# A hybrid decoder step on one Trainium2 core: the attention stage and the samples' decode attention put into one stated order of small pieces

## The chip, the cores and the metric

The program runs on 1 core of one Trainium2 chip. The metric is the device time of one execution in microseconds (us), lower is better. TensorE is PE in the profile (PEld is its weight load, which overlaps its matmuls), VectorE is DVE, ScalarE is ACT, GpSimd is POOL and SyncE, which here issues most of the DMAs, is SP.

## The reference

One inference step of a two-layer trunk for a prompt of 512 tokens and 8 samples of one token, with shared weights: layer 0 is native sparse attention, layer 1 an mLSTM. What matters here is layer 0:

```
h = rmsnorm(x);  q, kv, win, gates, z = split(h @ w_in)          # 16 heads of 64, 4 kv heads
o_c = softmax(q kc - slope*d) vc        # compressed keys (31 of the prompt, 63 of a sample)
o_s = softmax(q ks - slope*d, selected blocks) vs
o_w = softmax(q kw - slope*d, window 512) vw
o   = g0*o_c + g1*o_s + g2*o_w
x   = x + (o * silu(z)) @ w_out
```

For the prompt of 512 tokens all 8 selection blocks fall within the 16 that may be selected, so both the selection and the window branch are causal attention over 512 rows. A sample attends to 1024 rows out of paged memory (128 rows a page, 8 pages, found through a page table) in the selection branch and to 512 rows of a window cache in the window branch.

## The kernel before, in words

All is float32. A product that needs full accuracy is three float32r matmuls on a high and a low part (`mm3`, lines 255 to 258). `load_w` (271) is how a weight comes in: SP issues its DMA into one of 2 `wraw` buffers, ACT copies the high part (276), `lo_of` (253) subtracts it on DVE or POOL.

The stages of layer 0 are: the k and v projections with the samples' compressed keys (up to about 235 us), the q tiles (`q_tile`, 651), the gate tiles z (`z_tile`, 677, to about 331 us), the attention (331 to 524 us), the output projection (lines 1085 to 1101). PSUM has 8 banks: 2 named mm, 3 named s, 2 named t and 1 named d.

**The prompt's attention** is 32 units (line 992): 2 head pairs hp, 4 groups g, and 4 row blocks i in the order 1, 3, 0, 2, each with 128(i+1) keys, 2 branches and 2 heads. For each of these 4 combinations `sub_a` (915) makes the scores with two matmuls (926, 927) into an s bank, DVE adds the distance and takes the extreme (929), ACT takes the exponential (931). `stats` (935) makes the 4 factors on DVE. `sub_b` (941) scales the scores on DVE (945), transposes them on PE (949) into an s or a t bank and copies them to SBUF (951 on ACT, 953 on DVE). `sub_pv` (959) multiplies all with the values in one run of matmuls (974), 2(2i+3) of them, into an mm bank. After the fourth unit of a (hp, g), `finish` (982) applies z and splits the result. `pair_start` (862) makes the compressed branch of a (hp, g): 8 matmuls (870), a softmax on DVE and ACT, a multiply on the engine that `PMUL` names (888), 2 transposes (891).

The loop at 1002 writes this down by hand: in step k it alternates the four `sub_a` of unit k with the four `sub_b` of unit k-1, and puts the value run of unit k-2 after the second of them. The compiler's scheduler then orders the instructions of each engine, by priority. The value runs and the samples' runs have a raised priority (`burst`, 708) and stay behind the newest score product; the first matmul of a value run waits for all four copies of its unit (969 to 972).

**The samples' decode attention** is a generator (`decode`, 716) that the loop advances by one piece in most steps (`DECP`, 1025): 12 score pieces (774, 32 matmul instructions each), a softmax over 1536 columns (779 to 801), three pieces for the compressed and the new rows, 12 value pieces (806, 16 instructions each, after a transpose at 811, a copy at 814 and a zeroing on POOL at 813), and the closing (839 to 848). Each score or value piece needs a block of 1 MB in one of 2 `dk` buffers. `fetch` (693) has SP issue it: 8 DMAs of one page each, each after a read of the page table (`pages`, 406), or one DMA for a window block. Three score pieces come in the z stage, at k = 3, 5 and 7; the generator's opening (the samples' compressed branch) and the fetch of block 0 come at k = 1 there, behind the load of z weight 2.

SP's instructions are in the order of the program up to line 1106. The first two output weights are loaded in steps 26 and 28 (`WOP`, 1027). After the loop the samples' result is put into the 8 operands of the output projection, by 8 copies on ACT (1030) and 8 subtractions on DVE. Then ACT issues the four loads of x for the residual (1053).

A class `Plan` (144) is used by two later stages, from about 731 us on. `P.op(engine, us, due, fn, ...)` notes a piece of one engine with what it reads and writes, and `P.run(order)` calls the pieces in the order of a tuple of numbers, within a block in which the scheduler keeps that order on all five engines:

```
    def run(self, order):
        gone = set()
        for k in order:
            fn, deps = self.ops[k]
            assert deps <= gone, k
            gone.add(k)
            fn()
```

The us and due of a piece are kept out of the program: only the order remains.

Of the kernel before, what the change touches and what calls it, by code (L numbers as in the profile page):

```python
# [32 lines left out]
LO_S = "VVVVVVVVVVVVVVVV"  # L33
# [6 lines left out]
PMUL = "VGGVVVVV"  # L40
# [5 lines left out]
WOP = (26, 28)  # L46
DECP = (0, 1, 1, 0, 1, 1, 0, 1, 1, 0, 1, 1, 0, 1, 1, 0, 1, 1, 0, 1, 1, 0, 1, 1, 0, 1, 1, 0, 1, 1, 1, 0, 1)
SBUFS = 7
PTB = 8
BURST = 4000  # L50
# [15 lines left out]
CS0, CSP = 6.0, 10.0  # L66
ORDER0 = (
# [17 lines left out]
ORDER1 = (  # L85
# [55 lines left out]
class Plan:  # L141
# [27 lines left out]
    def run(self, order):  # L169
        assert sorted(order) == list(range(len(self.ops)))  # L170
# [3 lines that stand above are left out]
            assert deps <= gone, k  # L174
            gone.add(k)
            fn()

# [33 lines left out]
def step_kernel(ctx, tc, ap):  # L211
# [479 lines left out]


# [13 lines left out]
    tail = []  # L706

    def burst(head):

        ctx_ = ExitStack()  # L710
        if tail:
            ctx_.enter_context(tc.high_priority(offset=BURST))
            ctx_.enter_context(tc.issue_after(head or tail[-1]))
        return ctx_

    def decode():
# [16 lines left out]
        pcm = d1.tile([128, 128], F32, name="dpc")  # L733
# [25 lines left out]
        V.tensor_reduce(st[:, 3:5], sn, axis=AX.X, op=OP.add)  # L759

        nxt = fetch(0)
        for u in range(12):
            yield
            cur, nxt = nxt, fetch(u + 1)
            dst = db()
            cs = slice(0, 128)
            kt = cur.rearrange("p b (h t) -> p b h t", h=2)
            head = None
            for par in (1, 0):
                for hp in range(2):  # L770
                    for cg in (3, 2, 1, 0):
                        b = 2 * cg + par
                        with burst(head):
                            m = PE.matmul(dst[32 * cg:32 * cg + 32, cs], QZ[:, hp, b], kt[:, b, hp],
                                          start=par == 1 and hp == 0, stop=par == 0 and hp == 1)
                        head = head or m.ins
            V.tensor_add(PS[:, u * 128:(u + 1) * 128], PS[:, u * 128:(u + 1) * 128], dst[:, cs])
        mn = d1.tile([128, 4], F32, name="dmn")
        V.tensor_reduce(mn[:, 0:1], PS[:, 0:1024], axis=AX.X, op=OP.min)
        V.tensor_reduce(mn[:, 2:3], PS[:, 1024:1536], axis=AX.X, op=OP.min)  # L780
        V.tensor_tensor(mn[:, 0:1], mn[:, 0:1], st[:, 3:4], op=OP.min)
        V.tensor_tensor(mn[:, 1:2], mn[:, 2:3], st[:, 4:5], op=OP.min)
        sm = d1.tile([128, 4], F32, name="dsm")
        pnw = d1.tile([128, 2], F32, name="dpn")
        S.activation(PS[:, 0:1024], PS[:, 0:1024], AF.Exp, scale=-1.0, bias=mn[:, 0:1], accum_out=sm[:, 0:1])
        S.activation(PS[:, 1024:1536], PS[:, 1024:1536], AF.Exp, scale=-1.0, bias=mn[:, 1:2], accum_out=sm[:, 1:2])
        V.tensor_sub(pnw, mn[:, 0:2], st[:, 3:5])
        S.activation(pnw, pnw, AF.Exp)
        V.tensor_add(sm[:, 0:2], sm[:, 0:2], pnw)
        V.tensor_scalar(sm[:, 0:2], sm[:, 0:2], 1e-30, None, op0=OP.max)  # L790
        V.reciprocal(sm[:, 0:2], sm[:, 0:2])
        V.tensor_mul(sm[:, 0:2], sm[:, 0:2], GD[:, 1:3])
        V.tensor_mul(pnw, pnw, sm[:, 0:2])
        V.tensor_scalar(PS[:, 0:1024], PS[:, 0:1024], sm[:, 0:1], None, op0=OP.mult)
        V.tensor_scalar(PS[:, 1024:1536], PS[:, 1024:1536], sm[:, 1:2], None, op0=OP.mult)
        V.tensor_scalar(pcm[:, 0:64], pcm[:, 0:64], GD[:, 0:1], None, op0=OP.mult)
        V.tensor_copy(pcm[:, 64:128], pcm[:, 0:64])
        pno = d1.tile([128, 2, 8], F32, name="dpo")
        for i in range(2):
            V.tensor_scalar(pno[:, i], C("bmask"), pnw[:, i:i + 1], None, op0=OP.mult)  # L800

        po = db()

        def pv_mm(lhs, rhs, b, start, stop):
            cg, s_ = b % 4, b // 4
            return PE.matmul(po[32 * cg:32 * cg + 32, s_ * 256:s_ * 256 + 256], lhs, rhs, start=start and s_ == 0,  # L806
                             stop=stop, skip_group_check=True)

        def p_nat(src, n):
            pp = xb()  # L810
            PE.transpose(pp[0:n, 0:128], src, ident)
            d = dp.tile([128, 8, 32], F32, name="dpt", tag="dpt")
            G.memset(d, 0.0)
            V.tensor_copy(d[0:n, :, 0:16], pp[0:n, 0:128].rearrange("p (b h) -> p b h", b=8))
            return d

        pc_ = p_nat(pcm, 128)
        for s_ in range(2):
            for cg in range(4):
                b = s_ * 4 + cg  # L820
                r = slice(64 * (b % 2), 64 * (b % 2) + 64)
# [75 lines left out]
    for k in range(8):  # L897
# [3 lines left out]
        if k % 2:  # L901
            next(dec)
# [1357 lines left out]
```

## Time and profile before

| | |
|---|---|
| time, median of 3 runs (lowest to highest) | 1162.23 us (1158.26 to 1164.24) |
| the profiled execution | 1153.69 us, its span 1152.0 us |
| granted clock, mean over the span | 0.976 |
| PE busy | 1069.0 us, 93% of the span |
| PEld, DVE, ACT, POOL busy | 82%, 70%, 54%, 23% |
| moved by DMA | 197.20 MB, 171 GB/s |
| the attention stage | 331 to 524 us |

A busy PE isn't a PE at its peak: matmuls are pipelined, each is shown for some 0.27 us and more, and the next starts well before that ends. A short wait between two matmuls therefore doesn't show as idle time of PE; the weight loads (PEld) show it. The view of the waits names for each engine the line that sat idle and the one that ended it; "issue" is a wait that the profile doesn't explain.

### The profile page before, as it was taken

What the parts mean: (1) busy time and instruction counts of PE and PEld (TensorE: products, weight loads), DVE (VectorE), ACT (ScalarE), POOL (GpSimd) and SP (SyncE); (2) the same over time, 40 slices, a digit from 0 to 9 for tenths busy, and PEclk for the clock granted to TensorE, in tenths of its full rate; (3) what the DMA queues carried; (4) which work ended last, traced back from release to release, by engine and by line L of the source; (5) the groups of instructions that cost most, each with busy time, mean ns of one, the idle gap of its engine ahead of it and who ended that gap; (6) DMA issues with size and microseconds to landing.
All of it is one profiled execution on the core that took longest, in us unless ns stands there. A gap on an engine that the chain in (4) does not pass through costs nothing.

```text
span 1152.0 us, 24275 instructions
## 1 busy us (share of the span) xinstructions
PE 1069.0 (93%) x8673; PEld 939.0 (82%) x8673; DVE 806.9 (70%) x1972; ACT 617.4 (54%) x1304; POOL 262.8 (23%) x296
## 2 busy tenths in 40 slices
PE   5899999999998999998899899898989999999985
PEld 4899999999987767678898899688956677877885
DVE  6675564487567888785777667585666778778786
ACT  5533444444566767673444344566665656655544
POOL 5021212043200000111543222231231233322111
PEclk9998999999999999999999999899999999999998
DMA  6544455023434433525444333679868787978522
GB/s 214 170 152 151 125 163 161 30 60 127 145 93 131 138 93 117 191 90 181 132 141 138 129 115 127 219 172 308 284 227 294 255 285 251 341 239 310 180 80 90
DMA packets 124754, 197.20 MB, mean 171 GB/s; under 512 B 16205, under 2 KB 66254, under 8 KB 124378
## 3 DMA queue, kind: packets, MB, share of 16 engines
q1 hardware_dynamic: 115930, 180.52, 48.8%
q10 hardware_dynamic: 8704, 15.13, 3.6%
q8 instruction: 68, 1.11, 0.4%
q14 instruction: 52, 0.43, 0.1%
HBM read 145.89 MB, written 58.10 MB: 177 GB/s over the span
## 4 chain that ended last, share of the span: by engine, by line
PE 60%; DVE 15%; DMA 9%; ACT 8%; issue 5%; SPq 2%; POOL 0%; DVEq 0%; ACTq 0%; POOLq 0%
PE mm L256 11%; PE mm L258 11%; PE mm L257 10%; DMA wraw<-in_m_in 4%; PE mm L974 3%; PE s L1817 3%; PE d L1453 2%; ACT pt L951 2%; PE s L257 2%; PE s L258 2%; PE s L256 2%; ACT s L931 2%; ACT whi L276 1%; PE t L949 1%; PE d L806 1%
## 5 line engine op out<-in xcount | busy, mean ns | idle before, releaser
L256 PE MATMUL mm<-hhi,whi 128*128 128x260 f32 (+1 forms) x976 | 284.3, 291 | 18.6 <-ACT hhi L314 9.7
L258 PE MATMUL mm<-hhi,wlo 128*128 128x260 f32 (+1 forms) x976 | 279.8, 287 | 5.1 <-DVE wlo L253 5.1
L257 PE MATMUL mm<-hlo,whi 128*128 128x260 f32 (+1 forms) x976 | 279.1, 286 | 0.0
L256 PEld LDWEIGHTS mm<-hhi,whi 128*128 128x128 f32 (+1 forms) x976 | 185.6, 190 | 27.0 <-issue 11.0
L253 POOL TENSOR_TENSOR wlo<-wraw,whi 128x1024 fp32r<-128x1024 f32 (+2 forms) x57 | 116.9, 2051 | 332.9 <-ACT whi L276 188.3
L258 PEld LDWEIGHTS mm<-hhi,wlo 128*128 128x128 f32 (+1 forms) x976 | 185.5, 190 | 6.9 <-DVE wlo L253 6.7
L257 PEld LDWEIGHTS mm<-hlo,whi 128*128 128x128 f32 (+1 forms) x976 | 185.6, 190 | 0.5
L276 ACT ACTIVATE whi<-wraw 128x1024 fp32r<-128x1024 f32 (+2 forms) x62 | 61.6, 993 | 106.8 <-DMA wraw<-in_m_in 46.6
L1472 DVE SCALAR_TENSOR_TENSOR cs<-t,wk,cs 128x512 f32<-128x512 f32 x128 | 88.4, 744 | 13.7 <-PE t L1445 10.2
L257 PE MATMUL s<-plo,w1h 128*128 128x256 f32 x256 | 73.7, 288 | 4.4 <-DVE plo L253 4.2
L1467 ACT ACTIVATE cs<-cs,SBC 128x1024 f32<-128x1024 f32 x64 | 70.7, 1141 | 12.5 <-PE d L1453 12.5
L931 ACT ACTIVATE s<-s,mn 128x256 f32<-128x256 f32 (+3 forms) x128 | 70.9, 555 | 11.1 <-DVE mn L929 7.8
L253 DVE TENSOR_TENSOR wlo<-wraw,whi 128x1024 fp32r<-128x1024 f32 (+1 forms) x44 | 48.9, 1114 | 39.2 <-ACT whi L276 33.1
L256 PE MATMUL s<-phi,w1h 128*128 128x256 f32 x256 | 76.0, 297 | 0.0
L258 PE MATMUL s<-phi,w1l 128*128 128x256 f32 x256 | 72.8, 284 | 0.0
L929 DVE CUSTOM_DVE_ANT_0 s<-s,D 128x256 f32<-128x256 f32 (+3 forms) x128 | 61.3, 486 | 10.0 <-PE s L927 7.1
L256 PE MATMUL mm<-uh,whi 128*128 128x260 f32 x224 | 66.1, 295 | 0.3 <-ACT sq L1927 0.2
L253 DVE TENSOR_TENSOR plo<-praw,phi 128x1024 fp32r<-128x1024 f32 x31 | 40.4, 1305 | 34.7 <-ACT phi L426 21.5
L257 PE MATMUL mm<-ul,whi 128*128 128x260 f32 x224 | 63.5, 284 | 0.0
L258 PE MATMUL mm<-uh,wlo 128*128 128x260 f32 x224 | 63.5, 284 | 0.0
L257 PEld LDWEIGHTS s<-plo,w1h 128*128 128x128 f32 x256 | 48.9, 191 | 5.5 <-DVE plo L253 5.0
L926 PE MATMUL s<-KA,qst 128*128 128x256 f32 (+3 forms) x128 | 49.1, 387 | 1.4 <-DVE mn L929 1.1
(472 smaller groups left out, 2723.4 us busy)
## 6 DMA issues: line engine op xcount, KB each, us to landing
cs<-in_state_C SPq DMA_DIRECT2D x64, 512.0 KB, 5.3
o_cs<-cs SPq DMA_DIRECT2D x64, 512.0 KB, 4.3
praw<-in_cache SPq DMA_DIRECT2D x128, 128.0 KB, 2.4
dk<-in_cache SPq DMA_DIRECT2D x128, 128.0 KB, 2.3
wraw<-in_m_in SPq DMA_DIRECT2D x32, 512.0 KB, 4.5
wraw<-in_m_out SPq DMA_DIRECT2D x32, 256.0 KB, 3.8
wraw<-in_w_kv SPq DMA_DIRECT2D x11, 512.0 KB, 3.4
wraw<-in_w_q SPq DMA_DIRECT2D x8, 512.0 KB, 3.4
```

The source lines that it names most:

```text
L253: (eng or V).tensor_sub(out, src, hi.bitcast(F32))
L256: PE.matmul(out, whi, xhi, start=start, stop=False)
L257: PE.matmul(out, whi, xlo, start=False, stop=False)
L258: PE.matmul(out, wlo, xhi, start=False, stop=stop)
L276: S.activation(hi, raw, AF.Copy)
L926: PE.matmul(p[:, 0:n], q[:, h2, i * 128:(i + 1) * 128], KA[:, kh, o:o + n], start=True, stop=False)
L929: V.tensor_tensor_reduce(s[:, 0:n], p[:, 0:n], D0[:, 384 - 128 * i:512], SLOPES[4 * kh + g], CLAMP, op0=OP.add, op1=OP.min, accum_out=mn[: ...
L931: S.activation(s[:, 0:n], s[:, 0:n], AF.Exp, scale=-1.0, bias=mn[:, h2, br:br + 1], accum_out=sm[:, h2, br:br + 1])
L974: m = PE.matmul(po[64 * h2:64 * h2 + 64, ts], lhs, rhs, start=n == 0, stop=n == len(todo) - 1)
L1467: S.activation(ct, ct, AF.Copy, scale=SBC[:, hd, 0, b:b + 1])
L1472: V.scalar_tensor_tensor(ct[:, i], D["pb_", k], D["wk_", hd][:, 2 * kh + i, b:b + 1], ct[:, i], op0=OP.mult, op1=OP.add)
L1817: PE.matmul(st_out(hd, j), ct[:, ks], X["q"][:, 128 * j:], start=kt == 0 and j < 3, stop=kt == 3, skip_group_check=True)
```

## The change

The prompt's attention, the samples' attention from their score piece 3 on, the loads of the first two output weights and the samples' 16 closing operations become 1054 pieces: 345 of PE, 390 of DVE, 275 of ACT, 22 of POOL and 22 of SP. `ORDER0` states them in one sequence; the former `ORDER0` and `ORDER1` are now `ORDER1` and `ORDER2` and are not changed. `DECP`, `WOP`, `burst`, the raised priority and the added waits at the head of a value run are gone. `PMUL` gives two more of the eight multiplies of the compressed branch to POOL. The number of buffers, the matmuls and the operations stay as they are. The opening of the decode attention and the fetch of block 0 come before the z tiles, ahead of the load of z weight 1.

```diff
-PMUL = "VGGVVVVV"
+PMUL = "VGGVGVGV"
-WOP = (26, 28)
-DECP = (0, 1, 1, 0, 1, 1, 0, 1, 1, 0, 1, 1, 0, 1, 1, 0, ...
-BURST = 4000
+AB, AS, AV = 4.0, 1.0, 5.0
+AL = {0: 3.4, 1: 4.6, 2: 6.0, 3: 7.4}
+DL0, DS0, DP0, DPS = 0.0, 78.0, 90.0, 7.0
 ORDER0 = (
+    8, 948, 950, 912, 954, 11, 9, 14, 913, 12, 10, 15, 13, 16, 17, 914, 34, 18, 63, 35, 19, 43, 20, 36, 37, 44,
+    21, 45, 40, 24, 27, 22, 30, 0, 41, 23, 38, 42, 25, 28, 1, 31, 26, 29, 2, 69, 32, 39, 60, 33, 3, 61, 921, 46,
...
+class _Now:
+    def op(self, eng, us, due, fn, **kw):
+        fn()
...
+    def dec_load(P, u, due):
+        D["dk", u] = Tile_("dk")
+        def load():
+            D["dk_", u] = fetch(u)
+        pages_ = u % 12 < 8
+        P.op("SP", 9.4 if pages_ else 0.4, due, load, new=[D["dk", u]], mb=0.13 if pages_ else 1.05)
+    def dec_qk(P, u, due):
...
+        P.op("PE", 1.3, due, run, r=[t], new=[dst])
+        P.op("DVE", 0.2, due + 1.3, add, r=[dst], w=[("PS", u)])
...
-    dec = decode()
+    N = _Now()
+    dec_open()
+    dec_load(N, 0, 0)
     for k in range(8):
         if k < 7:
             wz.append(load_w(ap["w_z"][k + 1], 8, eng=E[LO_Z[k + 1]]))
         z_tile(k, wz[k])
-        if k % 2:
-            next(dec)
+        if k in (3, 5, 7):
+            u = k // 2 - 1
+            dec_load(N, u + 1, 0)
+            dec_qk(N, u, 0)
         if k == 6:
-            for _ in pair_start(0, 0):
-                pass
+            pair_start(N, 0, 0, 0)
...
+    def att_unit(P, hp, g, i, due):
...
+                P.op("PE", TA[n], d, prod, r=[qt], new=[pt_])
+                P.op("DVE", TT[n] + 0.01, d + 0.6, dist, r=[pt_] + ([] if f0 else [mn]), w=[(mn, key)],
+                     new=[st] + ([mn, sm] if f0 else []))
+                P.op("ACT", TE[n], d + 1.4, ex, r=[(mn, key)], w=[st, (sm, key)])
...
+        P.op("DVE", 0.26, b_ - 0.5, stats, r=[(sm, k_) for k_ in sp_], w=[sm], lock=True)
...
+                P.op("DVE", TS[n], d, scale, r=[sm], w=[st])
+                P.op("PE", 0.11 * (i + 1) + 0.02, d + 0.5, tr, r=[st], new=[pb_])
+                P.op("ACT" if PTC[2 * i + h2] == "S" else "DVE", TC[n], d + 1, copy, r=[pb_], new=[pt_])
...
+        P.op("PE", 0.228 * (2 * i + 3) + 0.15, b_ + AV, pv, r=list(pts.values()) + [D["ptc", hp, g]], w=[] if f else [po],
+             new=[po] if f else [])
...
-    for k in range(len(units) + 1):
...
+    P = Plan({"mm": 2, "s": 3, "t": 2, "d": 1, "dk": 2, "qo": 9, ...
+    for k, (hp, g, i) in enumerate(units):
+        if k % 4 == 0 and k + 4 < 32:
+            pair_start(P, *units[k + 4][:2], at_ + 6)
+        att_unit(P, hp, g, i, at_)
+        at_ += AL[i]
+    end_ = at_
+    for u in range(3, 12):
+        dec_load(P, u + 1, DL0 + 9.6 * (u - 3))
+        dec_qk(P, u, DL0 + 2 + 9.0 * (u - 3))
+    dec_soft(P, DS0)
+    dec_first(P, DS0 + 6)
+    for u in range(12):
+        if u < 11:
+            dec_load(P, 13 + u, DL0 + 9.6 * (u + 9))
+        dec_pv(P, u, DP0 + DPS * u)
+    dec_close(P, DP0 + DPS * 12 + 2)
+    for k in range(2):
+        wo_load(P, k, end_ - 20 + 8 * k)
...
+    for k in range(8):
+        P.op("ACT", 0.1, end_ + 2.5 + 0.2 * k, lambda k=k: samp_h(k), r=["us", D["uo", k]], w=[("uos", k)])
+        P.op("DVE", 0.08, end_ + 3 + 0.2 * k, lambda k=k: samp_l(k), r=["us", (D["uo", k], 1), ("uos", k)], lock=True)
+    with tc.manual_schedule(engines=every):
+        P.run(ORDER0)
```

What the sequence says can be read from the numbers, since pieces are numbered in the order in which they are noted. Counted in that way: the value run of a unit has 2 to 25 other PE pieces between itself and the last of the unit's transposes, 8 in the median; a unit's first transpose piece has 4 to 13 other PE pieces between itself and its last score product, 8 in the median. One of the three s banks is taken 192 times; 38 of these takes stand at most 5 places (of all engines) behind the piece that empties the bank, the median 7. The page blocks of the scores are fetched and used in the order 4, 7, 5, 6, 10, 8, 11, 9. The loads of output weights 0 and 1 stand behind the fetch of block 10, and ACT's copies of their high parts 12 and 21 PE pieces after these loads. The 8 ACT copies of the samples are the last ACT pieces, behind the split of the last unit.

## Rows read from the trace of the kernel before

**Rows 1.** Stages: us, busy PE, PEld, DVE, ACT, POOL, clock, DMA share, GB/s.

```profile
331.00:524.00 193.00, 175.17 (x1982) 138.91 (x1982) 154.29 (x637) 133.62 (x413) 13.17 (x19) 0.99 0.39 122
740.00:846.00 106.00, 100.42 (x786) 90.77 (x785) 68.17 (x127) 68.57 (x131) 25.53 (x32) 0.98 0.79 244
846.00:1075.00 229.00, 224.14 (x1306) 166.29 (x1305) 174.37 (x356) 137.24 (x223) 66.22 (x80) 0.99 0.84 284
```

**Rows 2.** Waits of PEld, 331 to 524: us in total, times, longest.

```profile
PEld mm L974 <- ACT pt L951: 14.1, 21, 1.1
PEld t L949 <- issue: 5.8, 16, 1.2
PEld s L926 <- DVE mn L929: 4.1, 13, 1.1
PEld t L949 <- DVE s L945: 3.9, 7, 1.6
PEld t L949 <- PE d L806: 2.5, 5, 0.8
```

**Rows 3.** The chain that ended last: start, us, what (count includes both passes).

```profile
392.01 0.50 ACT pt L951
392.55 2.19 PE mm L974 x36
394.74 1.01 PE d L774 x32
...
436.06 0.81 PE t L870 x8
...
445.54 1.00 PE d L806 x16
...
459.46 1.31 PE mm L974 x20
...
461.77 0.60 PE t L949 x4
```

**Rows 4.** Timeline of PE: score products of 256 and of 512 keys.

```profile
331.14 0.28 PE L927 MATMUL s<-KB,qst 128*128 128x256 f32 x1
...
331.37 0.28 PE L927 MATMUL s<-KB,qst 128*128 128x256 f32 x1
...
333.51 0.39 PE L927 MATMUL s<-KB,qst 128*128 128x512 f32 x1
...
333.96 0.40 PE L927 MATMUL s<-KB,qst 128*128 128x512 f32 x1
```

**Rows 5.** Groups of instructions, 331 to 524: busy, mean ns | idle before.

```profile
L256 PE MATMUL mm<-uo,whi 128*128 128x260 f32 x7 | 2.2, 310 | 0.0
...
L276 ACT ACTIVATE whi<-wraw 128x1024 fp32r<-128x1024 f32 x2 | 2.1, 1058 | 1.8 <-DMA wraw<-in_w_o 1.7
...
L1030 ACT ACTIVATE uo<-us 128x8 fp32r<-128x8 f32 x8 | 1.0, 196 | 0.0
```

**Rows 6.** Timelines of SP (merged issues) and of ACT: start, us.

```profile
263.08 11.81 SPq L274 DMA_DIRECT2D wraw<-in_w_z  x3
...
287.65 8.21 SPq L410 DMA_DIRECT2D dk<-in_cache  x8
...
395.81 78.09 SPq L410 DMA_DIRECT2D dk<-in_cache  x64
...
276.74 1.06 ACT L276 ACTIVATE whi<-wraw 128x1024 fp32r<-128x1024 f32 x1
```

**Rows 7.** DMA issues: KB each, median us from issue to landing.

```profile
dk<-in_cache SPq DMA_DIRECT2D x96, 128.0 KB, 2.3
...
wraw<-in_w_q SPq DMA_DIRECT2D x8, 512.0 KB, 3.4
```

**Rows 8.** Timeline behind the attention: ACT's queue, and PE.

```profile
524.56 1.79 ACTq L1053 DMA_DIRECT2D x<-in_xT  x4
...
528.88 0.39 PE L256 MATMUL mm<-uo,whi 128*128 128x260 f32 x1 [1.01 <-DVE x L1091]
```

More of the change, by code (lines that the diff above doesn't have):

```diff
@@ L772, in decode @@
                         b = 2 * cg + par
[L773 to L779, printed above, removed]
@@ L796, in decode @@
[L796 to L807, printed above, removed]
@@ new lines, in pv_mm, with p_nat, tr, zero @@
+    def pv_mm(lhs, rhs, b, start, stop):
+        cg, s_ = b % 4, b // 4
+        return PE.matmul(D["po_"][32 * cg:32 * cg + 32, s_ * 256:s_ * 256 + 256], lhs, rhs, start=start and s_ == 0,
+                         stop=stop, skip_group_check=True)
+    def p_nat(P, key, src, n, due, r):
+        pp, d = Tile_("t"), Tile_("dpt")
+        D["dpt", key] = d
+        X = {}
+        def tr():
+            X["pp"] = xb()
+            PE.transpose(X["pp"][0:n, 0:128], src(), ident)
+        def zero():
+            D["dpt_", key] = dp.tile([128, 8, 32], F32, name="dpt", tag="dpt")
+            G.memset(D["dpt_", key], 0.0)
+        def put():
+            V.tensor_copy(D["dpt_", key][0:n, :, 0:16], X["pp"][0:n, 0:128].rearrange("p (b h) -> p b h", b=8))
+        P.op("POOL", 0.32, due - 2, zero, new=[d])
+        P.op("PE", 0.13, due, tr, r=r, new=[pp])
+        P.op("DVE", 0.2, due + 0.4, put, r=[pp], w=[d])
@@ L896, in step_kernel, with f1 @@
-    dec = decode()
+        X = {}
+        pcm, s, mc, pp, ptc = Tile_("t"), Tile_("sc"), Tile_("mc"), Tile_("t"), Tile_("ptc")
+        D["ptc", hp, g], D["pov", hp, g] = ptc, Tile_("mm")
+        def f1():
+            q = qst[hp, g]
+            X["p"] = xb().rearrange("p (h i n) -> p h i n", h=2, i=4)
+            for h2 in range(2):
+                for i in range(4):
+                    PE.matmul(X["p"][:, h2, i], q[:, h2, i * 128:(i + 1) * 128], KQ[:, 2 * hp + h2], start=True,
+                              stop=True)
@@ new lines, in f_h, with f_l @@
+        def f_h():
+            uo[k] = qop.tile([128, 2, NTOK], F32R, name="uo", tag="qo")
+            S.activation(uo[k][:, 0, 0:512], X["u"], AF.Copy)
+        def f_l():
+            lo_of(uo[k][:, 1, 0:512], X["u"], uo[k][:, 0, 0:512], E[LO_UO[k]])
+        P.op("DVE", 0.6, b_ + AV + 2, f_u, r=[po], new=[u])
+        P.op("ACT", 0.5, b_ + AV + 3, f_h, r=[u], new=[o])
+        e = LO_UO[k]
+        P.op(EN[e], WLO[e][0], b_ + AV + 4, f_l, r=[u, o], w=[(o, 1)], lock=True)
+    units = [(hp, g, i) for hp in range(2) for g in range(4) for i in IORD]
@@ L1379, in head_factor @@
         V.tensor_mul(out, v, r)
-    EN = {"V": "DVE", "G": "POOL"}
-    WLO = {"V": (0.68, 1.23), "G": (1.28, 2.4)}
-    CTI = [Tile_("big") for _ in range(16)]
-    VTI = [[Tile_("big") for _ in range(4)] for _ in range(4)]
-    D = {}
     def head_open(P, hd, due):
@@ L1727, in step_kernel @@
     with tc.manual_schedule(engines=every):
-        P.run(ORDER0)
+        P.run(ORDER1)
     r1.close()
@@ L2121, in step_kernel @@
     with tc.manual_schedule(engines=every):
-        P.run(ORDER1)
+        P.run(ORDER2)
     kctx.close()
```

493 lines of the change are left out of this document (282 added, 211 removed), and 48 rows, old and new, of the table ORDER0.

## The prediction, made before the changed kernel ran

> **What bounds the kernel now.** I read the table of stages first. In the 193.0 us of the attention PE is busy 175.17, DVE 154.29, ACT 133.62, POOL 13.17 us, at a granted clock of 0.99 (the 2.4 GHz level) [rows 1]: no engine is full, and PE is the fullest. In the two stretches that already run in a stated order PE is busy 100.42 of 106.0 and 224.14 of 229.0 us [rows 1], 95% and 98%, against 91% here.
>
> Busy time hides short waits, so I count PE's work from the steps between starts. A value run takes 2.19 us for 9 pairs of matmuls and 1.31 for 5 [rows 3], 0.22 a pair and 0.21 on top: 0.87, 1.31, 1.75, 2.19 for the four row blocks, 6.12 together, 49.0 us for 8 groups. Four transposes take 0.60 us [rows 3], of which the last one's length, about 0.28 as in [rows 4], is pipeline: 0.11 a step, 320 of them 35.2 us. A score product of 256 keys takes 0.23 us from start to start, one of 512 keys 0.45 [rows 4]; I take 0.34 for 384 and, bounded above by the 256 and rounded up for the weight load, 0.25 for 128: 1.27, times 4 combinations and 8 groups 40.6 us. Seven openings of a group at 0.81 [rows 3] and two transposes make 7.2. Nine score pieces of the samples at 1.01 and twelve value pieces at 1.00 [rows 3] and a transpose make 9.1 and 13.3; the three small pieces, sized as value pieces, and the closing 3.8. Sum 158.2 us. 21 matmuls of the output projection also fell into the stage (7 on each of three lines [rows 5]), 2.5 us at 0.12, the step that the 256-key products show. So PE holds 160.7 us of work in 193.0, and **32.3 us is waiting and refilling**.
>
> The view of waits says for what: value runs for ACT's copies of the transposes 14.1 us, transposes for nothing the profile explains 5.8, score products for an s bank that DVE empties 4.1, transposes for DVE's scaling 3.9, transposes behind the samples' value pieces 2.5 [rows 2].
>
> A page of the Trainium skill speaks to the same headroom: Perfetto Trace Analysis, "Identifying the Most-Contended Engine", says that the busy share of matmuls is no good measure of how near TensorE is to its peak, and that the busy share of the weight loads is better. The busy row would leave at most 193.0 - 175.2 = 17.8 us to win, the page's measure 193.0 - 138.9 = 54.1 [rows 1]; the count above lies between.
>
> **The change, part by part.**
>
> *Value runs behind their copies.* Before, a run is put behind the newest score product and waits for all four copies. In the sequence it has 8 other PE pieces in front in the median; priced as above that is 4.2 us of PE work, at least 1.0 us for 31 of the 32 runs, and an ACT copy takes 0.50 us [rows 3]. So most of the 14.1 us goes. A wait of the weight load is partly covered by the matmul before it, so not all is won: bounds 7 (half) and 14.1, taken 12, nearer the row. What is late next is the s bank.
>
> *Transposes behind the scaling.* The first transpose of a unit has 3.8 us of PE work between itself and its last product (median), at least 1.9; exponential, factors and scaling fit. Of 3.9 us [rows 2] I take 2.5; bounds 0 and 3.9.
>
> *s and t banks.* The 4.1 and 2.5 us [rows 2] are about buffers whose number doesn't change. The samples' pieces are now spread one by one. Bounds: all 6.6 won, or as much lost again; taken 2 won, since the sequence leaves 7 places between release and take in the median. The unexplained 5.8 us I leave, at nothing.
>
> *SP's page blocks.* Blocks 4, 7, 5, 6 can be issued only one behind another: one took 8.21 us with nothing to wait for, 8 of them 78.09, 9.76 each with waits [rows 6], and a page lands 2.3 us later [rows 7]. PE has 8.9 us of work before it wants block 4 and 17.0 before block 7, SP needs 10.5 and 18.7 at least: 1.6 and 0.1 late, 4 together if SP takes 9.76 a block. In the second half six value blocks follow each other from the end of value piece 0 to the start of piece 7: 6 x 8.21 + 2.3 = 51.6 us (60.9 at 9.76) beside 53.5 us of PE work, which at the forecast pace takes 61. That covers it; without that cover it costs up to 7.4. Taken 2 lost, bounds 0 and 7.4.
>
> *Other new waits.* On queues kept in order a late piece holds all behind it, also what could run: behind ACT's copy of an output weight stand exponentials and copies that PE waits for. These loads now come 12 and 21 PE pieces ahead of their copy; before, ACT waited 1.7 us for them once [rows 5]. I take 2 for all such waits, bounds 0 and 5 (three of that size).
>
> *z stage.* The fetch of block 0 now stands ahead of z weight 1 on SP. Weight 0 was issued at 263.08 [rows 6]; 8.21 us of page issues later, at about 271.7, weight 1 follows and lands 3.4 us later (the like load [rows 7]) at 275.1, and its split began at 276.74 [rows 6]. So 1.6 us of cover: nothing. If the pages take 9.76 us, 0.1 is left; upper bound 1. The opening itself moves by one z tile beside PE's matmuls: nothing, bounds -1 and +1.
>
> *The two multiplies on POOL, the new names, the former orders as ORDER1 and ORDER2.* DVE and POOL have room [rows 1], the rest is unchanged: nothing, within 1 us either way.
>
> *Behind the attention.* ACT's 8 copies of the samples, 0.196 each [rows 5], now stand between the last unit's split and the four loads of x. These began at 524.56 and PE went on at 528.88, after the first sum with x [rows 8]; that moves by 8 x 0.196 = 1.6 us. The 21 matmuls that had filled gaps come here and fit into the wait. 1.7 lost, bounds 0 and 4.
>
> Sum: -12 - 2.5 - 2 + 2 + 2 + 1.7 = **-10.8 us**, the attention itself from 193 to about 181. The profiled execution, 1153.69 us, would become 1142.9. It lay below the three runs shown (median 1162.23); I carry the difference over to the median: 1162.2 - 10.8 = 1151.4, forecast **1151 us**.
>
> **The rivals.**
>
> *More goes than I take (chance 0.14).* If all named waits go (14.1 + 3.9 + 4.1 + 2.5 = 24.6) and only the tail is lost: -22.9, 1139 us. For it: DVE and ACT are under 80% busy, the ordered stretches hold PE at 95 to 98%. Against: the pages alone need 51.6 of the 53.5 us of PE work between value pieces 0 and 7.
>
> *The waits only change their names (0.18).* The sequence may wait for pages and for ACT as much as the old one did for copies; then 12 + 2.5 + 2 is met by 7.4 + 5 and 2.5 of the tail: -1.6, 1161 us. For it: the pages' small cover. This case also holds that the stated order comes out in practice much like the scheduler's.
>
> *Three s banks stop PE: slower (0.10).* The place is the score products and every second transpose, which share three banks, 192 takes in all; DVE or ACT must empty a bank first. Today 13 takes wait 4.1 us, 0.32 each [rows 2]. A scheduler could put other work in front at such a spot; a fixed PE queue can't. With 16.5 us won and 1.7 lost in the tail, it decides from 14.8 / 0.32 = 46 takes on; the 38 takes that stand within 5 places of the release are just short of that. If every second take waits, 96 x 0.32 = 31 us less the 4.1 of today: +12, 1174 us.
>
> The Trainium skill has a rule for this rival: Perfetto Trace Analysis, "Optimization Strategy", takes a gap that repeats over a stretch on the engine that should be full as a sign that SBUF or PSUM is short of room for the next tile, and no order adds room. The trace speaks mostly against it: the largest repeated gap is for data, 14.1 us, and the bank's is 4.1 [rows 2].
>
> **How the numbers follow.** The forecast has 0.58, its own range 1145 to 1157 (terms at their bounds, not all at once). About 0.5%, 6 us, is what a measurement of this kernel can tell from no change, so "same" is 1156.4 to 1168. Faster: the forecast, less its upper edge, and the fast rival: 0.71. Same: 0.19. Slower: 0.10. The range reaches from the fast rival, 1139, over the renamed waits to 1163; some 0.08 lies below and 0.12 above.
>
> **What would show it.** In the changed trace the attention should take 178 to 184 us with PE at 95% or more; the wait of value runs for ACT's copies should fall from 14.1 to under 3; the wait for s banks should stay under 6; SP's page issues should run nearly without a gap in the second half; the loads of x should be issued about 1.6 us later behind the last value run than now. I am wrong if the stage is above 188 us, or if waits of ACT or PE for a DMA come to more than 6 us in it, or if the bank waits pass 15.

## The result, and the profile of the changed kernel

The changed kernel took 1151.4 us in the median of 20 runs (1140.66 to 1159.37), the kernel before 1158.7 in 20 runs beside it (1154.05 to 1164.24): ratio 0.9938, 95% interval 0.9917 to 0.9959, so 4.8 to 9.6 us faster. Measured once more in other turns it gave 0.9938 again (0.9909 to 0.9967). The forecast of 1151 us hit the median, with some luck: it stood on three runs whose median lay 3.5 us above that of the 20. The gain that was forecast, 10.8 us, lies just outside the interval.

The profiled executions have spans of 1152.0 and 1148.6 us. All line numbers from here on are the changed kernel's, unless an experiment says otherwise. First the stretch from the first score product to the end of the last value run in the table of stages (columns as in [rows 1]), which answers to the first of [rows 1]:

```profile
333.10:516.10 183.00, 173.19 (x1965) 136.32 (x1961) 156.46 (x623) 131.15 (x405) 13.97 (x20) 1.00 0.42 128
```

The stage takes 183.0 us where it took 192.5 (330.9 to 523.4), and PE is busy 94.6% of it. The waits of the weight loads, answering to [rows 2]:

```profile
PEld s L1106 <- ACT pt L1153: 5.4, 11, 1.8
PEld s L1106 <- DVE mn L1114: 5.3, 14, 0.8
PEld mm L1174 <- issue: 3.4, 18, 0.3
PEld t L1148 <- issue: 3.1, 6, 1.8
PEld t L1148 <- ACT s L1119: 2.5, 4, 1.2
PEld t L1148 <- DVE s L1143: 2.4, 7, 0.6
PEld s L1148 <- DVE mn L1114: 2.4, 9, 0.5
```

The row of value runs (L1174) waiting for ACT's copies, 14.1 us before, is gone altogether. But three rows of score products and transposes waiting for an s bank now make 5.4 + 5.3 + 2.4 = 13.1 us; before, the one such row in [rows 2] was 4.1. What a weight load waits for may be hidden by the matmul still running, so the same view for the matmuls themselves, that is PE truly idle, in 331 to 524. Before:

```profile
PE mm L974 <- ACT pt L951: 7.8, 19, 0.8
PE t L949 <- DVE s L945: 3.8, 5, 1.3
PE d L774 <- DMA dk<-in_cache: 1.9, 1, 1.9
PE s L926 <- DVE mn L929: 1.1, 2, 0.8
```

and in the changed kernel:

```profile
PE t L1148 <- DVE s L1143: 3.0, 4, 1.6
PE s L1106 <- ACT pt L1153: 2.5, 3, 1.5
PE mm L313 <- DVE x L1329: 1.8, 1, 1.8
PE s L1106 <- DVE mn L1114: 1.5, 4, 0.5
PE t L1047 <- POOL sc L1042: 0.8, 1, 0.8
```

Of the 14.1 us, 7.8 had left PE idle. That is the lower figure, since idle time begins only at the modelled end of the matmul before: counted from the start of one matmul to the start of the next, each late start against the usual step to such a start, I estimate that the waits cost some 9 us. All of it is gone, and so are 1.9 us for a page. Come new are 2.5 us for banks that ACT empties, and 0.8 for a multiply that the change moved to POOL. The third row lies behind the stage. As a sum, PE's idle time in the stage fell from 192.5 - 175.2 = 17.3 us to 183.0 - 173.2 = 9.8.

Rows of the timeline tell of the places around it, the samples' opening among the z tiles and the end:

```profile
281.01 0.98 PE L776 MATMUL t<-KC,QZ 128*32 128x64 f32 x23 [1.84 <-DVE QZ L729]
...
519.08 2.62 ACTq L1291 DMA_DIRECT2D x<-in_xT  x4
...
523.89 0.39 PE L313 MATMUL mm<-uo,whi 128*128 128x260 f32 x1 [1.80 <-DVE x L1329]
```

and one of the view of waits, of ACT:

```profile
ACT whi L1213 <- DMA wraw<-in_w_o: 2.4, 1, 2.4
```

The opening, now directly behind the last q tile, makes PE wait 1.84 us for that tile's QZ, a wait that the kernel before hadn't. ACT waits 2.4 us for an output weight (1.7 in [rows 5]). The loads of x are issued 3.4 us behind the start of the last value matmul; before it was 1.6 ([rows 8], with the last value matmul at 523.0).

To compare runs I read four distances off each trace: from the first issue of a z weight to the first score product (z stage), from there to the start of the last value matmul (attention), from there to the first load of x, and from the first score product to the first sum with x. The clock is that granted in the attention.

| kernel | z stage | attention | to x load | to first sum | clock |
|---|---|---|---|---|---|
| before | 67.8 | 192.1 | 1.6 | 197.5 | 0.99 |
| changed | 69.3 | 182.6 | 3.4 | 190.3 | 1.00 |
| changed, again | 69.3 | 184.3 | 3.4 | 191.7 | 0.98 |
| opening back | 67.8 | 183.1 | 3.4 | 190.7 | 0.99 |
| no lead | 70.8 | 218.7 | 4.4 | 227.1 | 0.97 |
| samples free | 69.3 | 182.5 | 3.4 | 189.8 | 0.99 |
| before, half a unit | 67.8 | 196.1 | 1.6 | 201.7 | 0.99 |
| low parts on VectorE | 68.6 | 182.6 | 3.4 | 190.8 | 0.99 |
| weights late | 68.7 | 180.5 | 3.4 | 188.4 | 1.00 |
| samples' copies on VectorE | 70.7 | 182.6 | 3.8 | 191.2 | 0.99 |
| gate products on VectorE | 68.8 | 182.8 | 3.4 | 190.3 | 1.00 |
| stated on PE only | 68.6 | 182.2 | 3.4 | 189.9 | 0.99 |
| three repairs | 68.0 | 180.4 | 3.4 | 187.7 | 1.00 |
| repairs and tail | 67.8 | 181.8 | 2.3 | 188.9 | 1.00 |

By these marks the change gave 7.2 us between the first product and the first sum and lost 1.5 in the z stage: 5.7 us. The difference in the attention isn't one of clock: "opening back" and "samples free", which have the changed kernel's order there, took 183.1 and 182.5 us at the 0.99 of the kernel before.

### The profile page after: what moved, and what is told of

It reads as the page before. It is cut to its first block, busy times and chain, and to the rows that moved or that the text cites. A ratio compares the mean times of both kernels' runs of the same rounds, so it can differ in the third digit from the quotient of the medians.

```text
span 1148.6 us, 24240 instructions
## 1 busy us (share of the span) xinstructions
PE 1071.7 (93%) x8673; PEld 939.2 (82%) x8673; DVE 812.1 (71%) x1970; ACT 616.7 (54%) x1304; POOL 262.8 (23%) x298
## 4 chain that ended last, share of the span: by engine, by line
PE 32%; DVE 9%; DMA 8%; issue 3%; ACT 3%; SPq 1%; DVEq 0%; POOL 0%; ACTq 0%; POOLq 0%
PE mm L313 7%; PE mm L315 7%; PE mm L314 7%; PE s L2050 3%; DMA wraw<-in_m_in 3%; DMA zd<-zt 3%; PE d L1686 2%; ACT whi L333 1%; DMA wraw<-in_m_out 1%; DVE wlo L310 1%; PE t L2035 1%; PE mm L2025 1%; DVE sacc L358 1%; DVE VT L1458 1%; DVE hlo L372 1%
## 5 line engine op out<-in xcount | busy, mean ns | idle before, releaser
L313 PE MATMUL mm<-hhi,whi 128*128 128x260 f32 (+1 forms) x976 | 284.3, 291 | 18.2 <-ACT hhi L371 10.6
L313 PEld LDWEIGHTS mm<-hhi,whi 128*128 128x128 f32 (+1 forms) x976 | 185.8, 190 | 26.7 <-ACT hhi L371 10.6
L1119 ACT ACTIVATE s<-s,mn 128x512 f32<-128x512 f32 (+3 forms) x128 | 71.3, 560 | 26.5 <-DVE mn L1114 25.1
L1700 ACT ACTIVATE cs<-cs,SBC 128x1024 f32<-128x1024 f32 x64 | 70.9, 1143 | 15.7 <-PE d L1686 15.1
L1114 DVE CUSTOM_DVE_ANT_0 s<-s,D 128x512 f32<-128x512 f32 (+3 forms) x128 | 59.4, 486 | 8.5 <-PE s L1107 7.6
```

Of the source, the lines that this page charges most:

```text
L313: PE.matmul(out, whi, xhi, start=start, stop=False)
L1114: V.tensor_tensor_reduce(s[:, 0:n], X["p", key][:, 0:n], D0[:, 384 - 128 * i:512], SLOPES[4 * kh + g], CLAMP, op0=OP.add, op1=OP.min, accu ...
L1119: S.activation(s[:, 0:n], s[:, 0:n], AF.Exp, scale=-1.0, bias=X["mn"][:, h2, br:br + 1], accum_out=X["sm"][:, h2, br:br + 1])
L1700: S.activation(ct, ct, AF.Copy, scale=SBC[:, hd, 0, b:b + 1])
```

## The experiments

The theory: a value run had stood right behind its own copies in PE's queue; put several PE pieces later, it finds them done, and that is the gain. The rivals: the gain is that of a stated order as such, on all engines; and what was won at the runs is waited for elsewhere.

**The lead taken away.** The changed kernel with each of the 32 value runs moved in the stated order to right behind the last copy of its own unit (0 to 3 PE pieces lie between, instead of 2 to 25). In the list, for the first unit, copies 23, 26, 29, 32 and run 33:

```diff
-... 26, 29, 2, 69, 32, 39, 60, 33, 3, 61, ...
+... 26, 29, 2, 69, 32, 33, 39, 60, 3, 61, ...
```

> The changed kernel, all in its stated order on all five engines, but each of the 32 value runs is put right behind the last copy of its own unit: 0 to 2 PE pieces stand between the unit's last transposes and its run, where the changed kernel has 2 to 25 (mostly 5 to 15). Theory (the gain is the lead of the copies over the run): PE waits for ACT's copies ahead of the runs again, 8 to 14 us by the rows of the kernel before (14.1), and the stage from the first score product to the end of the last run goes from 183 to 190 to 195 us. Rival (the gain comes from the order being stated, not from the lead): the stage grows by 3 us at most and no row of value runs waiting for copies above 4 us is there.

Measured: 1189.0 us, ratio 1.0267 (1.0218 to 1.0315). The stretch in the table of stages:

```profile
333.70:552.80 219.10, 185.92 (x1983) 143.44 (x1979) 158.60 (x619) 132.33 (x405) 13.54 (x20) 0.97 0.35 107
```

and the waits of PE's matmuls, of ACT and of VectorE in it (its line numbers are 4 lower; L1170 are the value runs):

```profile
PE mm L1170 <- ACT pt L1149: 11.6, 18, 2.0
PE t L1144 <- DVE s L1139: 6.3, 9, 1.0
PE s L1144 <- DVE mn L1110: 5.0, 7, 2.2
PE mm L1170 <- DVE pt L1151: 4.1, 6, 1.8
...
ACT s L1115 <- DVE mn L1110: 46.7, 42, 3.7
...
DVE s L1110 <- PE s L1103: 35.4, 27, 3.7
```

The waits for copies are back and larger than in the kernel before: 11.6 + 4.1 = 15.7 us of PE idle, where there it was 7.8. The theory holds in kind, but its size was wrong: 36 us more, not 7 to 12. The last two rows fit this reading: a run that waits in a fixed queue also holds the score products behind it, so VectorE waits 35.4 us for products (7.6 in the changed kernel) and ACT 46.7 for VectorE (25.1), and the next copies are later still. Some of it, up to 0.03 x 219 = 6.6 us, is clock, 0.97 against 1.00. The rest of the list was not adapted to the moved runs, so the 36 us are the price in this list, not that of every order without the lead.

**The lead alone.** The kernel before, one line changed (its own line numbers):

```diff
-            if br == 0 and pend:
+            if br == 1 and pend:
                 flush()
```

> The kernel before with one line changed: a unit's value run is written behind the fourth of the next unit's transposes instead of the second, half a unit later. Nothing is stated beyond what was. Theory (a lead of the copies is what counts): the wait of the value runs for ACT's copies falls from 14.1 to below 7 us and the stage from 192.6 to 184 to 188 us. Rival (a scheduler that picks the order from its own estimates puts the run where it likes, or the eight pt buffers, now all held, stop the next copies): the stage stays at 191 us or above, with the waits under another name.

Measured: 1166.5 us, ratio 1.0051 (1.002 to 1.0083), slower; attention 196.1 us. Waits of PE's matmuls:

```profile
PE t L949 <- DVE s L945: 9.7, 9, 2.1
PE s L949 <- DVE s L945: 3.8, 6, 1.1
PE s L949 <- ACT pt L951: 1.6, 3, 0.6
```

No wait for copies at the value runs is left that the view lists, but the transposes now wait 9.7 + 3.8 = 13.5 us for VectorE's scalings, 3.8 before. Here the rival was right: the wait only changed its name. By these rows a later run is not enough; what PE comes to in its place must be ready too.

**The order stated for PE alone.**

```diff
-    with tc.manual_schedule(engines=every):
+    with tc.manual_schedule(engines={mybir.EngineType.PE, mybir.EngineType.SP}):
         P.run(ORDER0)
```

> The changed kernel with the same list of pieces, but stated for PE and SP alone: VectorE, ACT and POOL are left to the scheduler, as all four engines but SP were in the kernel before. Theory A (what counts is that PE's queue has other pieces between a unit's copies and its value run; the other engines can take theirs in any sensible order): the stage from the first score product to the last value run is 181 to 186 us. Theory B (VectorE's and ACT's queues are as much a part of it, since a copy that stands behind the wrong exponential comes late however PE is ordered, which is what the half-unit lead alone, 196.1 us, points to): 188 us or more, and PE's waits for ACT's copies and VectorE's scalings are above 10 us.

Measured: 1150.5 us, ratio 0.9900 (0.9861 to 0.9939); attention 182.2 us. Waits of PE's matmuls, and the two longest of ACT:

```profile
PE t L1148 <- DVE s L1143: 4.1, 5, 1.3
PE s L1106 <- DVE mn L1114: 2.7, 3, 2.0
PE t L1148 <- ACT pt L1153: 1.6, 1, 1.6
...
ACT pt L1153 <- PE t L1148: 20.2, 20, 2.4
ACT s L1119 <- DVE mn L1114: 17.7, 23, 1.9
```

Theory A. With VectorE, ACT and POOL left to the scheduler the stage is as short as with all five stated; PE's waits are spread otherwise (banks 2.7 instead of 4.0, scalings 4.1 instead of 3.0), and so are ACT's (17.7 us for VectorE instead of 25.1, 20.2 for transposes instead of 13.4). So of "all five engines" in the change, stating PE's sequence, with SP's, was enough; SP's instructions were in a fixed order before, too. But the scheduler was given the calls in the order of the list, and it kept most of it: instruction by instruction, some 530 of VectorE's 623 and 375 of ACT's 405 stand in the stated sequence. How a freer order of these two would do was not tried.

**The opening put back.**

```diff
-    dec_open()
-    dec_load(N, 0, 0)
     for k in range(8):
...
         z_tile(k, wz[k])
+        if k == 1:
+            dec_open()
+            dec_load(N, 0, 0)
```

> The changed kernel with one step taken back: the samples' opening (its score products on the compressed cache, and the first page load) stands again behind the second z tile, not ahead of the first. Theory: ahead of the first tile the opening's products follow the last q tile at once, and PE waits for that tile's QZ on VectorE (1.84 us, once, in the changed kernel; no such row in the kernel before). With other tiles in between the wait is gone: the first score product starts at about 331.1 instead of 333.1 us, the attention stage keeps its 183 us, the whole is 2 us shorter. Rival: the opening costs PE the same wherever it stands, and the first score product stays within 0.5 us of 333.1.

Measured: 1150.1 us, ratio 0.9903 (0.9871 to 0.9935). The z stage is 67.8 us, that of the kernel before, and the wait for QZ is gone. The kernels that leave the opening ahead have 68.6 to 69.3 at full clock (in those at 68.6 to 68.8 PE waits 1.2 to 1.3 us at a later piece of the opening instead): it costs 0.8 to 1.5 us, 1.5 in the two profiles compared. Times can't show so little. The first score product started at 326.6, not 331.1, since this execution was 5 us ahead before the z stage, for a reason given at the end.

**Output weights 0 and 1.** In the changed kernel their high and low parts come at 379 to 387 us, amid the scalings; before they came at 486 to 495. What POOL, VectorE and PE did there in the changed kernel:

```profile
380.35 2.37 POOL L310 TENSOR_TENSOR wlo<-wraw,whi 128x1024 fp32r<-128x1024 f32 x1 [14.08 <-ACT whi L1213]
384.50 2.42 POOL L310 TENSOR_TENSOR wlo<-wraw,whi 128x1024 fp32r<-128x1024 f32 x1 [1.77 <-ACT whi L1213]
...
381.52 1.23 DVE L1023 TENSOR_SCALAR mc<-mc 128x8 f32<-128x8 f32 x1
...
384.22 3.77 DVE L1143 TENSOR_SCALAR s<-s,sm 128x512 f32<-128x512 f32 x4
...
381.41 0.33 PE L1106 MATMUL s<-KA,qst 128*128 128x128 f32 x1 [1.50 <-ACT pt L1153]
...
387.73 0.63 PE L1148 MATMUL t<-cst,s 128*128 128x128 f32 x4 [1.61 <-DVE s L1143]
```

A scaling of 128x8 elements, 0.17 us in the median of its 8, takes 1.23 and ends with POOL's first pass (380.35 + 2.37 = 382.72); four scalings, 1.67 in the second profile below, take 3.77 beside POOL's second pass. In the second profile of the same kernel other instructions were hit:

```profile
380.10 2.36 POOL L310 TENSOR_TENSOR wlo<-wraw,whi 128x1024 fp32r<-128x1024 f32 x1 [13.26 <-ACT whi L1213]
384.24 2.56 POOL L310 TENSOR_TENSOR wlo<-wraw,whi 128x1024 fp32r<-128x1024 f32 x1 [1.78 <-ACT whi L1213]
...
380.38 2.23 DVE L1143 TENSOR_SCALAR s<-s,sm 128x256 f32<-128x256 f32 x1
...
384.51 2.32 DVE L1131 TENSOR_SCALAR sm<-sm 128x4 f32<-128x4 f32 x1
...
387.51 0.69 PE L1148 MATMUL s<-cst,s 128*128 128x128 f32 x2 [2.24 <-DVE mn L1114]
```

Even 4 elements a row, 0.17 us in the median, took 2.32, until POOL was through. The Trainium skill has this on its page SBUF — State Buffer, section "Who interferes with whom": VectorE's tensor_scalar can take the port pair that it shares with GpSimd, and the second comer is fully blocked until the first has finished, not slowed. Both traces agree, down to the ends.

Two kernels took this apart. The low parts on VectorE:

```diff
-LO_O = "GGVVGGGG"
+LO_O = "VVVVGGGG"
```

> The changed kernel with the low parts of output weights 0 and 1 on VectorE instead of POOL, at the same two places of the order. In the changed kernel they run on POOL for 2.37 and 2.42 us from 380.35 and 384.50, and beside the second one the scaling of four 512-wide tiles on VectorE takes 3.77 us where it takes 1.80 elsewhere, one of them 2.58; PE waits 1.81 us for it. Theory (POOL's pass over 128x1024 shuts VectorE out for as long as it runs): without it the longest scaling falls from 2.58 to below 1 us, PE's wait of 1.81 at that place goes, and VectorE's own 2 x 1.2 us cost less than that: the stage goes from 182.6 to 180.5 to 182 us. Rival (VectorE has no room there either): the stage is 182.6 to 185 us, with waits of PE for VectorE of the same size a little earlier or later.

Measured: 1145.5 us, ratio 0.9872 (0.9801 to 0.9943). The long scalings at that place are gone; the longest of all, 1.30, stood beside POOL's pass for a pair's low part. In the 28 us from 44 us behind the first product PE was busy for 26.4 us (24.4 in the changed kernel), but at a granted clock of 0.94 in just these 28 us, where the same work takes longer. The attention took 182.6: this run alone doesn't decide. Then the six pieces of the two weights moved back in the order, the low parts still on POOL:

```diff
-... 930, 1031, 213, 1034, 214, ...
+... 930, 213, 214, ... 757, 992, 1031, 1034, 752, ...
-... 250, 1032, 274, ... 270, 1033, 257, ... 232, 1035, 276, ... 277, 1036, 256, ...
+... 792, 795, 1032, 798, ... 791, 1033, 809, ... 820, 835, 1035, 842, ... 825, 1036, 1014, ...
```

> The changed kernel with the loads, high parts and low parts of output weights 0 and 1 moved some 100 us back in the stated order, to about where the kernel before had them (high and low parts around 490 us instead of 379 to 387), the low parts still on POOL. Theory: ACT's wait for the weight's transfer (2.4 us at 379.2, with the copies of attention queued behind it) and POOL's shutting out VectorE are what keeps PE idle in the stretch from 379 to 403 us, where PE works 20.4 of 24 us and waits 1.76, 0.76 and 1.81 us in single waits; without them PE works 22.9 or more there and the stage falls by 2.5 to 4 us, less up to 1.5 for POOL's passes at the new place: 179 to 181.5 us. Rival (the order is tuned to the place, and the waits for banks come anyway): the stage stays at 182 to 184 us.

Measured: 1147.9 us, ratio 0.9916 (0.9880 to 0.9951); attention 180.5 us at clock 1.00, 2.1 less than the changed kernel at the same clock. In the same 28 us PE was busy for 27.4 us, also at 1.00, ACT's wait for the weight is gone, and the waits of weight loads for banks fell from 13.1 to 10.6 us. PE's own waits for banks:

```profile
PE s L1106 <- DVE mn L1114: 1.6, 4, 0.5
...
PE s L1106 <- ACT pt L1153: 0.6, 1, 0.6
```

The theory holds, the 1.5 us for POOL's passes at the new place included. Value run by value run, this kernel is 3.5 us ahead of the changed one from 57 us behind the first product on, and 2.1 from 174 on. Between the two marks, beside POOL's pass from 488.93 to 491.31, stand

```profile
490.29 1.30 DVE L1131 TENSOR_SCALAR sm<-sm 128x4 f32<-128x4 f32 x1 [0.39 <-ACT s L1119]
...
492.74 0.63 PE L1148 MATMUL t<-cst,s 128*128 128x128 f32 x4 [1.29 <-DVE s L1143]
```

So POOL's pass, by these rows, shut VectorE out at the new place too, for a shorter time. Behind the attention the run fell back by a clock of 0.89 in one stretch of 15 us, so its time shows it less.

**The gate products of pairs 4 and 6 back on VectorE.**

```diff
-PMUL = "VGGVGVGV"
+PMUL = "VGGVVVVV"
```

> The changed kernel with the gate products of pairs 4 and 6 put back from POOL to VectorE (the engine string of the kernel before). In the changed kernel PE waits 1.01 us, once, for such a product, one that took 0.96 us on POOL. Theory: that wait goes and the two products cost VectorE 0.7 us with room for it, so the stage falls by 0.5 to 1 us to 181.6 to 182.1. Rival: VectorE is the engine that PE waits for most, and the stage is the same or up to 1 us longer, 182.6 to 183.6.

Measured: 1153.6 us, ratio 0.9932 (0.9898 to 0.9966); attention 182.8. The rival: the move to POOL cost nothing and gave nothing that a stage can show.

**The samples' copies at the end.** First they were taken out of the stated order:

```diff
-    P.op("DVE", 0.12, end_ + 2, samp, r=[("OS", 0), ("OS", 1)], w=["us"])
...
         P.run(ORDER0)
+    samp()
+    for k in range(8):
+        samp_h(k)
+        samp_l(k)
     actx.close()
```

(and the 17 pieces from 1037 on leave the list).

> The changed kernel with the samples' gate product and their 16 small copies taken out of the stated order and left to the scheduler behind it, as in the kernel before. Theory: ACT's 8 small copies (0.89 us with what stands before them) hold back the x loads, which ACT issues behind them; from the end of the last value run to PE's going on is 7.8 us in the changed kernel and 5.5 before, and it falls to about 6 here: 1.6 to 2.3 us of the whole. Rival: the x loads wait for the memory of the attention's buffers, not for ACT, and the 7.8 us stay within 0.5.

Measured: 1149.7 us, ratio 0.9913 (0.9882 to 0.9945). The scheduler left the eight copies where they had been, ahead of the loads of x; the loads came 3.4 us behind the last value matmul as before. The rival's number, but nothing was told apart. So the copies went to VectorE:

```diff
-        S.activation(uo[k][:, 0, 512:520], D["us"][:, k], AF.Copy)
+        V.tensor_copy(uo[k][:, 0, 512:520], D["us"][:, k])
```

> The changed kernel with the samples' eight high copies on VectorE instead of ACT. (Taking them out of the stated order left them ahead of the x loads on ACT, so that run did not tell.) Theory: ACT issues the x loads right behind its copy of the last pair, at about 1.5 us behind the last value run instead of 3.0, and PE goes on 6.2 to 6.6 us behind the last value run instead of 7.8: 1.2 to 1.6 us of the whole. Rival (the loads wait for the memory of the attention's buffers): they issue at 2.5 us or later and PE goes on at 7.3 us or later.

Measured: 1155.1 us, ratio 0.9951 (0.9917 to 0.9984). VectorE's last low part and ACT's loads:

```profile
520.38 0.70 DVE L310 TENSOR_TENSOR uo<-us,uo 128x8 fp32r<-128x8 f32 x8
...
521.24 2.31 ACTq L1291 DMA_DIRECT2D x<-in_xT  x4
```

ACT was free and the loads still waited, until the samples' last low part was through (520.38 + 0.70 = 521.08). They go out 0.16 us behind it, and so they did in the changed kernel, where the row of VectorE is `518.22 0.70` and the loads start at 519.08. So it isn't ACT's queue that holds them but the end of the samples' work. The rival's numbers came; that the loads wait for memory which the samples still hold, no row shows. In the kernel before the samples were done at 518.0 us, 5 ahead of the last value matmul; the change put them last.

**The repairs together.** The opening back, the low parts on VectorE, and the weights' high and low parts some 30 pieces later (1032, 1033, 1035, 1036; their loads stay).

> The changed kernel with three repairs at once: the samples' opening behind the second z tile (alone: z stage 69.3 to 67.9 us), the low parts of output weights 0 and 1 on VectorE (alone: PE works 23.5 of 24 us in 379 to 403 instead of 20.4), and their high and low parts some 30 pieces further back in the order, so that ACT does not wait 2.4 us for the first transfer. Theory: the losses are separate and add: z stage 67.9, attention 180 to 181 us, both against 69.3 and 182.6; 3 us less than the changed kernel, a ratio of 0.990 to 0.993 to the kernel before where the changed kernel has 0.993 to 0.996. Rival (what is repaired in one place is waited for in the next): the attention stays at 182 to 183.

Measured: 1144.0 us, ratio 0.9869 (0.9843 to 0.9896), beside 1155.2 and 0.9938 (0.9909 to 0.9967) for the changed kernel in the same turns:

> The changed kernel unaltered, in the same turns as the two kernels of repairs, to compare them on one chip: ratio to the kernel before 0.992 to 0.996, z stage 69.3 and attention 182.6 us again, with PE's wait of 1.8 us for a scaling beside POOL's second low part.

The z stage is 68.0 and the attention 180.4 us: 1.3 and 2.2 less than the changed kernel's first profile, as the theory said. That makes 3.5 us. The ratio came out lower than expected for that; the two intervals allow a gain of 1.5 to 14 us over the changed kernel, and what is above 3.5 no row shows. This kernel beats both. The control's attention came to 184.3, not 182.6, at a clock of 0.98, and its single wait at POOL's second pass was the 2.24 us shown above instead of 1.61. A part of what is above 3.5 may be such clock: of the eight profiles of kernels with the output weights early, six were granted 1.2 GHz for 3.4 us or twice that, starting 50 to 55 us behind the first product, within or right behind PE's waits there; of the three with the weights late none was. (The 23.5 us that the expectation gives for the low parts on VectorE are no measure: they are from a stretch of absolute time, in which that run was 7.7 us further on.)

Last, on top of the repairs, the end of the order: the samples' last value run and transposes earlier, their product and seven of the eight copies ahead of the last pair's, and the eighth low part no longer tied to the pair's:

```diff
-... 877, 896, 880, 1020, 899, ... 1024, 882, 907, 1025, 1029, 1022, 908, 1030, 1023, 1027, 909, 1028, 910, 1037, ...
+... 1020, 877, 896, 880, ... 1029, 1030, 882, 1027, 1028, 1037, 908, 1038, 1040, ... 1051, 909, 910, 1052, 1053, 911,
```

> The kernel of the three repairs with the last 80 pieces of the stated order put otherwise: the samples' last value run and its four transposes some 10 pieces earlier, and the samples' gate product and copies of seven of the eight tiles ahead of the last pair's. The two runs on the samples' copies showed that ACT's x loads wait for the last of these copies, on whatever engine it is: 3.4 us behind the start of the last value matmul in the changed kernel (3.8 with the copies on VectorE), 1.6 in the kernel before, where the samples were done 6 us earlier. Theory: the x loads come at 1.6 to 2.4 us, the first residual add follows 1 to 1.8 us sooner and PE's wait for it (1.8 us) falls below 1: another 1 us or so. Rival (the transposes and outputs pulled forward hold PE back ahead of the last value runs): the stage grows by as much, and the two kernels are equal within 0.5 us.

Measured: 1148.0 us, ratio 0.9906 (0.9870 to 0.9942). The loads of x came at 2.3 us, but PE's first matmul behind them:

```profile
520.93 0.58 PE L313 MATMUL mm<-uo,whi 128*128 128x260 f32 x1 [2.38 <-DVE x L1330]
```

It waited 2.38 us, longer than the 1.40 in the kernel of the three repairs. The loads follow the last value matmul by 1.1 us less, but the attention grew by 1.4: counted from the first score product they went out at 184.1 us instead of 183.8, and the first sum started at 188.9 instead of 187.7. The rival, if slower than its "equal within 0.5 us". The attention falls back only in its last 7 us, where the pieces pulled forward stand.

## Why the prediction was right, and where it wasn't

*Value runs behind their copies: the mechanism right, the size off.* Forecast 12 of the 14.1 us. The wait is gone to the last tenth, and taking the lead away brings it back. But PE had been idle for only 7.8 of them (some 9 by the estimate from start to start). The step that failed is "taken 12, nearer the row": the prediction said that the matmul before covers part of a weight load's wait, and then took nearly all of it. Its own lower bound, 7, was the nearer end, and the view of PE's own waits would have told.

*Transposes behind the scaling.* Forecast 2.5 won; PE's own row went from 3.8 to 3.0 us. The 1.61 of one wait in it are POOL's shutting out; without them 2.4 would have been won.

*Banks: the sign wrong.* Forecast 2 won with waits under 6; they rose to 13.1 on the weight loads, and on PE from 1.1 to 2.5 + 1.5 = 4.0, some 3 lost. The third rival, that a fixed queue can't put other work in front, was right in kind and far off in price: 34 takes, 0.39 us each, not 96. With the output weights moved away the 13.1 become 10.6, and PE's own 4.0 become 0.6 + 1.6 = 2.2. So nearly 2 of the 3 us were lost behind the weights, and the banks as such cost 1.1. Why the rest waits, and whether a fourth s bank would end it, wasn't tried: the eight banks are all given out.

*SP's page blocks.* Forecast 2 lost; PE's 1.9 us for a page went to nothing. The issue of the 64 value pages took 88.8 us, not nearly gapless as expected (78.09 in [rows 6]), and PE never waited for one.

*Other new waits.* Forecast 2 lost, with ACT's copy of an output weight named: ACT waited 2.4 us there and PE 1.50 behind it, which are among the 2.5 just counted for banks. What the prediction didn't see is that the low parts moved with the copies to where VectorE scales: moving the weights away won 2.1 us in all, 3.5 at the place that they left.

*The z stage.* Forecast nothing, bounds -1 to +1. It lost 1.5: the prediction looked at SP's queue and at the opening's own length, not at what the opening reads, the QZ of the tile just ended. That a step loses its cover when it is moved next to its producer was the missing line.

*The two multiplies on POOL.* Forecast nothing; nothing: PE's 0.8 us behind one of them gave no shorter stage when they were moved back.

*Behind the attention.* The loads of x came 1.8 us later, forecast 1.6, but through the samples' end, not through ACT's eight copies. And PE paid nothing for it: it idled 0.79 + 1.01 = 1.80 us there before and 1.80 after, since output-projection matmuls that had filled gaps in the attention (21, 2.5 us by the prediction's count) now fill this wait.

Put together: 7.8 and 1.9 us of idle time won at copies and pages and 0.8 at scalings, some 3 lost at banks and 0.8 at POOL, and small single waits; in all PE idles 7.5 us less. The stage is 9.5 us shorter, the other 2 (2.5 by the prediction's count) by those matmuls that now come later; then 1.5 lost ahead of it. Too high a gain at the copies and too dark a view of the pages partly met, and the sum was nearer than its terms. That the forecast time met the median is the luck named at the start. The case "waits change their names" describes one half of what happened at the banks, and all of what the lead alone did.

## What to carry to other kernels

Read a wait twice, on the weight loads and on the matmuls: what can be won lies nearer to the second. In a queue that keeps its order, give every consumer a few pieces of lead over its producer, and check each moved piece for what it now stands next to: its producer, or a pass on POOL beside VectorE's scalings. Stating PE's order may be all that is needed; here the engines that feed it could be left to a scheduler that got their calls in the same order.

## What the runs showed of the hardware that was not expected

*A lost lead multiplies.* 15.7 us of PE waiting for copies in the kernel without the lead went with a stage 36 us longer, and VectorE and ACT, which make the next copies, waited longer for PE and for each other.

*Part of the scatter between executions has a place.* It is the stretch from 60 to 120 us, long before anything that the change touches, in the table of stages. The changed kernel:

```profile
60.00:120.00 60.00, 57.73 (x439) 57.16 (x438) 38.45 (x65) 22.86 (x49) 12.19 (x9) 0.91 0.45 142
```

and the one with the opening back:

```profile
60.00:120.00 60.00, 58.28 (x483) 57.85 (x483) 42.56 (x70) 26.28 (x55) 14.72 (x11) 1.00 0.47 148
```

PE is as busy in both, as it was in the 60 us ahead (42.85 and 42.87), and gets through 439 and 483 matmuls. One was granted the 2.4 GHz level throughout, the other a mean of 0.91, so part of the stretch at 1.2 GHz: 0.09 x 60 = 5.4 us, and it is 5 us behind from then on (first z weight at 263.8 and 258.7 us). The kernels "low parts on VectorE" and "weights late" also had 1.00 in their profiles, the kernel before and the others 0.89 to 0.91. Why the clock fell in some and not in others no row shows. So differences of a few microseconds were read from distances within the stage, with the clock beside them, and the medians are given with their intervals.
